# Hybrid decoder layer: where the gated norm's token scale is applied

## The chip, the cores and the metric

The kernel runs on one NeuronCore of a Trainium2 chip. The metric is the device time of one execution in microseconds (us); less is better. The engines are named as the profile names them: PE (TensorE: matmuls; PEld is its weight load), DVE (VectorE), ACT (ScalarE), POOL (GpSimd) and SP (SyncE, which here only issues DMAs). [...] The runs of the kernel before took 1358.45, 1358.78 and 1361.12 us, so the median is 1358.78 us.

## The reference, cut to what matters

One decoder layer is computed for 256 prompt tokens and 8 x 4 sample tokens, 288 columns in all, with D = 2048 features and fp32 accuracy. The part around the change is this (cut from the reference):

```python
h = rmsnorm(x, norm1) * (1 + sc1) + sh1
u_pool, z, xbc, dt_raw = split(h @ w_in)        # 512, 1536, 2560, 24 columns
pool_out = pool_mixer(u_pool)                   # 512 wide: window means minus the token, a 128x128 map per group
y = ssd(xbc, dt_raw) * silu(z)                  # 1536 wide
y = y * rsqrt(mean(y * y) + EPS) * ssd_norm     # gated RMSNorm: one factor for each token
mix = concat([pool_out, y]) @ w_out             # 2048 -> 2048
x = x + g1 * mix
h2 = rmsnorm(x, norm2) * (1 + sc2) + sh2        # then the gated MLP with a depthwise conv, and a final norm
```

The factor `rsqrt(mean(y*y)+EPS)` is one number per token. The matmul contracts over features, so that factor can be applied to `y` ahead of the projection, or to the projection's share of `y` behind it. The share of `pool_out` must not get it.

## The kernel before, in words

Features lie on the 128 partitions and the 288 tokens along the free axis, so an activation is 16 tiles of 128x288 (`KT = 16`) and a product is made per output tile `m` over the 16 tiles `k`. Every large product is made from fp32 operands that are each cut into two fp32r parts: `split` (L292) makes the parts `whi` (ACT, a cast, L288) and `wlo` (DVE, a subtraction, L290) of a weight block of eight `k`, and `mm3` (L300) issues three matmuls per `k`: high by high (L302), high weight by low activation (L303), low weight by high activation (L304). The activation's parts are `xhi[k]` and `xlo[k]`; `new_operand` takes 16 slots for each, so the tile `k` of a new operand takes the slot of the tile `k` of the operand before it, once the last matmul that reads it is through.

Weights come through SP as 512 KB blocks (`load`, L266), each into one of eight `raw` slots in this stage; a load waits on SP until a slot is free, and everything behind it on SP waits too. Blocks of the modulation weights (`raw_adap`, `ada_part_units`, L404) come through the same slots; their small matmuls (`adap`, L331) are filler work for PE, emitted by `pull(adas, ...)`.

The order of the work is the program's order, changed by the framework's scheduler: for every engine it makes one fixed list, from the program order, priorities (`tc.high_priority` in `split`) and its own estimate of when an operand is ready. On the chip each engine then works through its list and waits at its head for semaphores.

The stages around the change are these. The loop at L1047 makes the columns of `w_in` for `z` and for the last two pooling groups: `("uz", m)` for m = 10 to 15, then 1 and 0 (`ULATE`). Each unit of it is two `k` (`YK = 2`, six matmuls). Between units it steps the generators of other work: `late` (pooling, `pool_units`, L863), `adas`, and `back`, which holds the last parts of the state-space mixer (`ssd3`) and then `y_norm` (L902). `outputs` (L812) leaves the gated `y` in `zy[g]` (three tiles for each of four groups) and adds its squares on POOL into `ssq` (L839). `y_norm` sums `ssq` over the partitions by matmuls with ones (`ysum`, L240), takes the root and the reciprocal (L246, L247), spreads the result over the partitions by matmuls (`pbrstdy`, L253), copies it to SBUF (`rstdy`, L260), and multiplies all of `zy` by it (L908: three groups on DVE, one on POOL).

Behind that loop the weights of the first output tile are split, the pooling is finished, and the new operand `mix` is written: `mixh` on ACT with the gain `ssd_norm` as scale (L1081), `mixl` on DVE (L1082), for the 12 tiles of `y`; `mix_pool` (L1073) does it for the four pooling tiles. The projection runs over k in the order `MIXK`: 4 to 15 (the tiles of `y`), then 3, 2, 1, 0 (pooling). The loop at L1132 then makes 16 output tiles (`project_units`, L308; the PSUM tile `mm_out` is one of three buffers of `pm`). `residual` (L1095) adds the gated tile to `x` on DVE (256 prompt columns in one instruction, L1096; 32 sample columns, L1099) and POOL (L1102); `squares` starts the next norm. `x` is loaded again, four tiles at a time, by SP at L1135. Small PSUM tiles come from `aux`, four buffers.

The scratch pool `mx` (`zy`, `pout` and the rest) is closed at L1086, and `ff`, which holds `x`, takes its place; a tile of `ff` waits for the tiles of `mx` that lay there.

Of the kernel before, what the change touches and what calls it, by code (L numbers as in the profile page):

```python
# [18 lines left out]
P = 128  # L19
D = 2048  # L20
KT = D // P
# [39 lines left out]
HB = [(0, 3), (3, 3), (6, 2)]  # L61
KGROUPS = [(0, 1), (1, 1), (2, 2), (4, 4), (8, 4), (12, 4)]
MIXK = list(range(4, KT)) + UEARLY + ULATE
TW = (5, 3)
FK = 3
DGROUPS = [(0, 15), (15, 14), (29, 14)]
# [97 lines left out]
def kernel(ctx: ExitStack, tc, ins, outs):  # L164
# [14 lines left out]
    def aux(name):  # L179
        return px.tile([P, 512], F32, tag="aux", name=name)  # L180
# [708 lines left out]
        yield  # L889

    def uz_units(m):
        for ps in project_units(("uz", m), KT):
            yield
        if m < 4:
            nc.scalar.copy(upp[:, m, 15:15 + NP], ps[:, 0:NP])
            nc.scalar.copy(ups[:, m, :, 15:19], samp(ps[:, NP:N]))
        else:
            g, t = divmod(m - 4, 3)
            nc.scalar.activation(zy_of(g)[:, t, :], ps[:, :N], AF.Silu)
            zdone.add((g, t))  # L900

    def y_norm():  # L902
        psq = aux("ysum")
        col_sums(psq, ssq, ones[:, 0:1], True, True)
        rstdyp, rstdy = rstd_of(psq, NH * 64, "rstdy")
        yield
        for g in range(4):
            (nc.gpsimd if g == 3 else nc.vector).tensor_tensor(zy[g], zy[g],  # L908
                                    (rstdy if g else rstdyp).unsqueeze(1).to_broadcast([P, 3, N]), ALU.mult)
            yield  # L910


    def chain(*gens):
# [133 lines left out]
    for m in list(range(4 + 3 * ZEARLY, 16)) + ULATE:  # L1047
        for _ in uz_units(m):
            n += 1
            for gn in late.values():  # L1050
                pull(gn, 0.5)
            pull(adas, RA2 / AY)
            pull(back, RB2 if n <= zlast else RB3)
            if n == zlast:
                drain(back)
                back = chain(ssd3, y_norm())
        if m < 4:
            late[m] = pool_units(m)
            next(late[m])
    pull(adas, TA / AY)  # L1060
    for h, (_, n) in enumerate(_halves(KT)):
        ready[("out", 0, h)] = split(load(("out", 0, h)), 0, n * P, f"out_0_{h}")
    for gn in late.values():
        drain(gn)
    drain(back)
    npl = kp.tile([P, 4, 135], F32, tag="hmod", name="npl", bufs=2)
    nc.gpsimd.tensor_copy(npl[:, :, 0:15], upp[:, :, NP:15 + NP])
# [9 lines left out]
    for g in range(4):  # L1077
        for t in range(3):
# [2 lines left out]
            nc.scalar.activation(xhi[0][k], zy[g][:, t, :], AF.Identity, scale=gv)  # L1081
            nc.vector.scalar_tensor_tensor(out=xlo[0][k], in0=zy[g][:, t, :], scalar=gv,  # L1082
                                           in1=xhi[0][k].bitcast(F32), op0=ALU.mult, op1=ALU.subtract)
    for g in MIXK[12:]:
        mix_pool(g)
    mx_ctx.close()  # L1086
    ff = ctx.enter_context(tc.tile_pool(name="ff", bufs=1, reuse_waits="tile"))
    w2 = ctx.enter_context(tc.tile_pool(name="w2", bufs=1, reuse_waits="tile"))
    shift(w2, 192)
    x = ff.tile([P, KT, N], F32, name="x")  # L1090


    rt = [kp.tile([P, N], F32, tag="ssx", name="rt2")]

    def residual(ps, part, m):  # L1095
        nc.vector.scalar_tensor_tensor(out=x[:, m, 0:NP], in0=ps[:, 0:NP], scalar=ada[:, part, m, 0:1],  # L1096
                                       in1=x[:, m, 0:NP], op0=ALU.mult, op1=ALU.add)
        t = kp.tile([P, NB, NL], F32, tag="rsd", name=f"rs{part}_{m}", bufs=2)
        nc.vector.tensor_tensor(t, samp(ps[:, NP:N]),  # L1099
                                ada[:, part, m, 1:NC9].unsqueeze(2).to_broadcast([P, NB, NL]), ALU.mult)  # L1100
        xs = samp(x[:, m, NP:N])
        (nc.vector if m == KT - 1 else nc.gpsimd).tensor_tensor(xs, xs, t, ALU.add)  # L1102

    def squares(m, name):
        sq = kp.tile([P, N], F32, tag="xsq", name=f"sq{name}_{m}", bufs=2)
# [26 lines left out]
    for m in range(16):  # L1132
        if m in XM:
            sl = slice(4 * XM.index(m), 4 * XM.index(m) + 4)
            nc.sync.dma_start(x[:, sl, :], ins["x"][:, sl, :])  # L1135
        if m == 5:
            wp[0].add(w2, RAW2, SPLIT2)
        for i, ps in enumerate(project_units(("out", m), KT, order=MIXK)):
            if m == KT - 1 and i == 5:
                all_but_last("ssum2")  # L1140
        residual(ps, 2, m)
        squares(m, "a")
        pull(adas, (1 + (m >= 14 - ADA_OUT)) / AY)
        if m == 13:
            drain(adas)
# [20 lines left out]
    stf = ff.tile([P, FT, NB, 2], F32, name="stf")  # L1166
    nc.gpsimd.dma_start(stf, ins["st_ffn"])
    nff = ff.tile([P, FT, 18], F32, name="nff")
    NG = 2 + NP + NB * 6
    acts = {}  # L1170

    def up_pair(j):
# [124 lines left out]
def _layout(inp):  # L1297
    f = {k: np.asarray(v) for k, v in inp.items()}
    dt = f["w_in"].dtype
    xa = np.concatenate([f["x_prompt"][0], f["x_sample"].reshape(NS, D)], 0)  # L1300
    ca = np.concatenate([f["c_prompt"], f["c_sample"]], 0)
    r = {"x": _ftile(xa.T), "c": _ftile(ca.T)}

    early, vec = np.zeros((P, NE), dt), np.zeros((P, NV), dt)

    def put(o, a, to=vec):
        a = _ftile(a)
        a = a.reshape(P, -1)
        to[:, o:o + a.shape[1]] = a

    put(V_N1, f["norm1"][0], early); put(V_BADA, f["b_ada"][0], early)
    put(V_N2, f["norm2"][0]); put(V_NF, f["norm_f"])
    perm = np.concatenate([np.arange(t * P, t * P + P) for t in PERM])
    put(V_CW, f["conv_w"][0].T[perm]); put(V_CB, f["conv_b"][0][perm])
    put(V_SN, f["ssd_norm"][0]); put(V_PS, f["pool_scale"][0])
    put(V_FW, f["ffn_conv_w"][0].T); put(V_FB, f["ffn_conv_b"][0])
    put(V_D, np.repeat(f["d_skip"][0], 64))
    vec[:NH, V_DTB] = f["dt_bias"][0]
    vec[:NH, V_AL] = f["a_log"][0]
    r["early"], r["vec"] = early, vec  # L1320

    k = vec
    i = np.arange(P)
    early[:, K_ID:K_ID + P] = np.eye(P)
    k[:, K_TRI:K_TRI + 2 * P] = np.tile(i[:, None] <= i[None, :], (1, 2))
    l32, m32 = np.arange(32)[:, None], np.arange(32)[None, :]
    same = l32 // NL == m32 // NL
    k[:32, K_BT4:K_BT4 + P] = np.tile(same & (l32 <= m32), (1, 4))
    k[:32, K_BO4:K_BO4 + P] = np.tile(same, (1, 4))
    k[:, K_SEL:K_SEL + 32] = np.tile(np.eye(32), (4, 1))  # L1330
    k[:, K_MLO] = np.where(i // 64 == 1, -1.0, 0.0)
    k[:, K_MHI] = np.where((i // 32) % 2 == 1, -1.0, 0.0)
    k[:, K_BM4:K_BM4 + NB] = (i[:, None] % 32) // NL == np.arange(NB)[None, :]
    for g in range(4):
        k[:, K_RC + 16 * g:K_RC + 16 * g + 16] = 1.0 / np.minimum(np.arange(16) + 1, 2 << g)
    early[::32, K_S4] = 1.0
    early[:, K_S2:K_S2 + 64] = np.tile(np.eye(64), (2, 1))

    sc = _ftile(f["state_conv"][0].transpose(2, 0, 1)[perm]).reshape(P, -1)
    sp = _ftile(f["state_pool"][0].transpose(2, 0, 1)).reshape(P, -1)  # L1340
    r["st"] = np.ascontiguousarray(np.concatenate([sc, sp], 1))
    r["st_ffn"] = _ftile(f["state_ffn"][0].transpose(2, 0, 1))
    r["pool_w"] = np.ascontiguousarray(f["pool_w"][0].transpose(1, 0, 2))
    h = f["state_ssm"][0].reshape(NB, 4, HG, 64, P)
    r["h0"] = np.ascontiguousarray(h.transpose(0, 4, 1, 2, 3)).reshape(NB, P, 4, G6)

    w = np.empty(_STREAM.size, dt)

    def tiles(mat):
        return mat.reshape(mat.shape[0] // P, P, mat.shape[1] // P, P)  # L1350

    wa = f["w_ada"][0].reshape(KT, P, 6, KT, P)
    wi = f["w_in"][0]
    wuz = tiles(wi[:, 0:2048])
    wx = tiles(wi[:, 2048:4608])
    wx = np.concatenate([wx[:, :, PERM], wuz[:, :, UEARLY + list(range(4, 4 + 3 * ZEARLY))]], 2)
    wdt = wi[:, 4608:].reshape(KT, P, NH)
    wo, wu, wd = tiles(f["w_out"][0])[MIXK], tiles(f["w_up"][0]), tiles(f["w_down"][0])
    full = {"uz": (wuz, 0), "out": (wo, 0), "gate": (wu, 0), "val": (wu, FT)}
    for key in _STREAM.order:  # L1360
        o, cols = _STREAM.items[key]
        kind = key[0]
        if kind == "ada":
            k0, gk = KGROUPS[key[1]]
            per = RAWC // (256 * gk)
            s = wa[key[2] * per:(key[2] + 1) * per, :, 0:2, k0:k0 + gk]
            s = s.transpose(1, 0, 2, 3, 4)
        elif kind == "dt":
            s = wdt.transpose(1, 0, 2)
        elif kind == "adap":  # L1370
            s = wa[key[2], :, key[1], 8 * key[3]:8 * key[3] + 8]
        elif kind == "xbc":
            ks, ms = _xbc_chunks(key[1])[key[2]]
            s = wx[ks][:, :, ms].transpose(1, 2, 0, 3)
        elif kind == "upk":
            s = wu[key[1]][:, [m for j in range(FK) for m in (j, FT + j)]]
        elif kind == "down":
            k0, nk = DGROUPS[key[1]]
            a, n = _halves(nk)[key[3]]
            s = wd[k0 + a:k0 + a + n, :, key[2]].transpose(1, 0, 2)  # L1380
        else:
            mat, m0 = full[kind]
            a, n = _halves(KT)[key[-1]]
            s = mat[a:a + n, :, m0 + key[1]].transpose(1, 0, 2)
        w[o:o + P * cols] = s.reshape(-1)
    r["wflat"] = w
    return r
# [45 lines left out]
```

## Time and profile before

| What | Value |
|---|---|
| median of three runs | 1358.78 us |
| the profiled execution's own time | 1359.14 us |
| its span, first to last instruction | 1357.2 us |
| PE busy | 1340.9 us, 99% |
| DVE, ACT, POOL busy | 808.8, 580.3, 223.8 us |
| mean granted PE clock | 0.995 |
| DMA moved | 323.18 MB, mean 238 GB/s |

The profiled execution took 1359.14 us, 0.36 us over the median; 1.94 us of it lie outside the span. In the views of the profile a row has a start in us from the span's start, a duration in us, an engine, a line of the kernel, an operation and its tiles. Square brackets behind a row give the idle time ahead of it and what ended that. "PEclk" is the share of full clock that PE was granted. Times that a row gives for a group (x16) run from the first start to the last end.

### The profile page before, as it was taken

The numbers are of one execution on the slowest core, as the hardware profiler recorded it, in microseconds if no ns is written. First come the engines' busy times: TensorE is split into PE (matmuls) and PEld (weight loads), VectorE is DVE, ScalarE is ACT, GpSimd is POOL, SyncE is SP. The second block draws the span as 40 slices with busy tenths as digits, with TensorE's granted clock in tenths as the row PEclk, the third lists the DMA queues.
The fourth block names the chain that finished last, engine by engine and source line by source line (L and its number), as shares of the span: only waits on it lengthen the run. The fifth ranks groups of instructions, "written<-read, shape, count | busy, mean of one in ns | idle before, by whom it ended". The sixth has DMA issues, their size and how long they took to land.

```text
span 1357.2 us, 26159 instructions
## 1 busy us (share of the span) xinstructions
PE 1340.9 (99%) x10517; PEld 1249.0 (92%) x10517; DVE 808.8 (60%) x1348; ACT 580.3 (43%) x911; POOL 223.8 (16%) x435
## 2 busy tenths in 40 slices
PE   9999999999999999999999999999999999999997
PEld 8889997776779889999999999999999999999997
DVE  5675568778564348645565455656554556566553
ACT  5343244577543335534443334443433334444452
POOL 0000012123121213111211001311220011132221
PEclk9999999999999999999999999999999999999999
DMA  9999768878878878787555555655555555566541
GB/s 371 405 408 365 257 245 320 341 263 296 301 278 321 323 263 261 244 288 272 184 184 184 162 180 183 201 190 184 176 186 167 186 188 192 187 205 191 181 120 70
DMA packets 97481, 323.18 MB, mean 238 GB/s; under 512 B 10768, under 2 KB 19920, under 8 KB 97360
## 3 DMA queue, kind: packets, MB, share of 16 engines
q1 hardware_dynamic: 93600, 310.79, 66.1%
q0 software_dynamic: 3184, 9.69, 2.0%
q8 instruction: 82, 1.34, 0.4%
q10 hardware_dynamic: 576, 1.03, 0.2%
q14 instruction: 39, 0.32, 0.1%
HBM read 309.78 MB, written 10.39 MB: 236 GB/s over the span
## 4 chain that ended last, share of the span: by engine, by line
PE 74%; DVE 1%; issue 0%; POOL 0%; ACT 0%; DVEq 0%; POOLq 0%
PE mm_down L303 7%; PE mm_down L302 7%; PE mm_down L304 7%; PE mm_val L303 6%; PE mm_gate L303 6%; PE mm_gate L302 6%; PE mm_val L304 6%; PE mm_gate L304 6%; PE mm_val L302 6%; PE adap L331 3%; PE mm_out L302 3%; PE mm_out L303 3%; PE mm_out L304 3%; PE mm_up L303 1%; PE mm_up L302 1%; PE mm_up L304 1%
## 5 line engine op out<-in xcount | busy, mean ns | idle before, releaser
L303 PE MATMUL mm_down<-al,whi_down 128*128 128x288 f32 x688 | 202.5, 294 | 0.0
L302 PE MATMUL mm_down<-ah,whi_down 128*128 128x288 f32 x688 | 202.4, 294 | 0.0
L304 PE MATMUL mm_down<-ah,wlo_down 128*128 128x288 f32 x688 | 202.0, 294 | 0.0
L303 PE MATMUL mm_gate<-h2l,whi_gate 128*128 128x288 f32 x640 | 188.8, 295 | 0.0
L303 PE MATMUL mm_val<-h2l,whi_val 128*128 128x288 f32 x640 | 188.8, 295 | 0.0
L304 PE MATMUL mm_val<-h2h,wlo_val 128*128 128x288 f32 x640 | 188.7, 295 | 0.0
L304 PE MATMUL mm_gate<-h2h,wlo_gate 128*128 128x288 f32 x640 | 188.6, 295 | 0.0
L302 PE MATMUL mm_gate<-h2h,whi_gate 128*128 128x288 f32 x640 | 188.5, 294 | 0.0
L302 PE MATMUL mm_val<-h2h,whi_val 128*128 128x288 f32 x640 | 187.7, 293 | 0.0
L290 DVE TENSOR_TENSOR wlo_gate<-raw_gate,whi_gate 128x1024 fp32r<-128x1024 f32 x80 | 98.2, 1229 | 136.5 <-ACT whi_gate L288 136.3
L290 DVE TENSOR_TENSOR wlo_down<-raw_down,whi_down 128x1024 fp32r<-128x1024 f32 x96 | 107.5, 1120 | 116.9 <-ACT whi_down L288 116.9
L288 ACT CAST whi_down<-raw_down 128x1024 fp32r<-128x1024 f32 x96 | 92.5, 964 | 167.0 <-PE mm_down L303 117.8
L288 ACT CAST whi_gate<-raw_gate 128x1024 fp32r<-128x1024 f32 x80 | 84.2, 1054 | 159.7 <-PE mm_gate L303 66.9
L288 ACT CAST whi_val<-raw_val 128x1024 fp32r<-128x1024 f32 x80 | 84.2, 1053 | 120.8 <-issue 101.6
L302 PE MATMUL xbc<-h1h,whi_xbc 128*128 128x288 f32 x448 | 133.4, 301 | 0.8 <-ACT h1h L452 0.7
L303 PE MATMUL xbc<-h1l,whi_xbc 128*128 128x288 f32 x448 | 132.0, 296 | 0.0
L304 PE MATMUL xbc<-h1h,wlo_xbc 128*128 128x288 f32 x448 | 130.0, 295 | 0.0
L302 PEld LDWEIGHTS mm_down<-ah,whi_down 128*128 128x128 f32 x688 | 129.2, 188 | 0.0
L303 PEld LDWEIGHTS mm_down<-al,whi_down 128*128 128x128 f32 x688 | 129.1, 188 | 0.0
L304 PEld LDWEIGHTS mm_down<-ah,wlo_down 128*128 128x128 f32 x688 | 129.0, 188 | 0.0
L302 PEld LDWEIGHTS mm_gate<-h2h,whi_gate 128*128 128x128 f32 x640 | 120.3, 188 | 5.0 <-ACT ah L1198 3.4
L302 PEld LDWEIGHTS mm_val<-h2h,whi_val 128*128 128x128 f32 x640 | 120.3, 188 | 0.0
(325 smaller groups left out, 2983.4 us busy)
## 6 DMA issues: line engine op xcount, KB each, us to landing
raw_adap<-wflat SPq DMA_DIRECT2D x128, 512.0 KB, 6.1
raw_gate<-wflat SPq DMA_DIRECT2D x80, 512.0 KB, 3.5
raw_val<-wflat SPq DMA_DIRECT2D x80, 512.0 KB, 3.9
raw_ada<-wflat SPq DMA_DIRECT2D x64, 512.0 KB, 9.6
raw_xbc<-wflat SPq DMA_DIRECT2D x50, 512.0 KB, 9.1
raw_down<-wflat SPq DMA_DIRECT2D x48, 512.0 KB, 3.6
raw_out<-wflat SPq DMA_DIRECT2D x32, 512.0 KB, 7.4
raw_down<-wflat SPq DMA_DIRECT2D x32, 384.0 KB, 3.1
```

The source lines that it names most:

```text
L288: yield nc.scalar.copy(hi[:, :n], raw[:, a:a + n])
L290: yield hi, lo, nc.vector.tensor_tensor(lo[:, :n], raw[:, a:a + n], hi[:, :n].bitcast(F32), ALU.subtract)
L302: nc.tensor.matmul(ps, whi[:, w], bh, start=first, stop=False)
L303: nc.tensor.matmul(ps, whi[:, w], bl, start=False, stop=False)
L304: nc.tensor.matmul(ps, wlo[:, w], bh, start=False, stop=last)
L331: nc.tensor.matmul(ps[32 * j:32 * j + 32, :nb], sc_c[:, k, :], raw[:, c:c + nb], start=(k == 0), stop=(k == KT - 1), tile_position=(0, 32 ...
```

## The change

`y_norm` goes. The operand `mix` is made from the unscaled `zy`, with only the gain `ssd_norm`. The sum of squares, the root and the spreading of the token factor (the first half of `y_norm`) are issued inside the first output tile, behind its fourth unit; the last pooling work and the four `mix_pool` behind its second unit. Each output tile now accumulates in two PSUM tiles: the first 12 of its 16 `k` (the features of `y`) in `pz` from `pm`, the last four (pooling) in `pp` from `aux`. When the 12 are through, `out_norm` multiplies `pz` by `rstdy` on DVE into an SBUF tile and adds that to `x` by `residual`; when the tile is through, `residual` runs a second time for `pp`. The number of matmuls stays the same. The last `("uz", 0)` tile walks its `k` in the order `MIXK`, so that the slots of h1's tiles 4 to 15 become free first, and its weights are laid out in that order on the host. The first output tile is issued ahead of `mx_ctx.close()`, and with it ahead of the first load of `x`.

```diff
+NZ = 12
     def uz_units(m):
-        for ps in project_units(("uz", m), KT):
+        for ps in project_units(("uz", m), KT, order=MIXK if m == ULATE[-1] else None):
             yield
-    def y_norm():
-        psq = aux("ysum")
-        col_sums(psq, ssq, ones[:, 0:1], True, True)
-        rstdyp, rstdy = rstd_of(psq, NH * 64, "rstdy")
-        yield
-        for g in range(4):
-            (nc.gpsimd if g == 3 else nc.vector).tensor_tensor(zy[g], zy[g],
-                                    (rstdy if g else rstdyp).unsqueeze(1).to_broadcast([P, 3, N]), ALU.mult)
-            yield
...
                 drain(back)
-                back = chain(ssd3, y_norm())
+                back = ssd3
...
-    for gn in late.values():
-        drain(gn)
     drain(back)
...
-    for g in MIXK[12:]:
-        mix_pool(g)
+
+    def out_units(m):
+
+        pz = pm.tile([P, 512], F32, tag="mm", name=f"mm_out_{m}")
+        pp = aux(f"mm_outp_{m}")
+        for h, (k0, n) in enumerate(_halves(KT)):
+            hi, lo = ready.pop(("out", m, h), None) or split(load(("out", m, h)), 0, n * P, f"out_{m}_{h}")
+            for i in range(n):
+                k = k0 + i
+                mm3((pz if k < NZ else pp)[:, :N], hi, lo, i, xhi[0][MIXK[k]], xlo[0][MIXK[k]],
+                    k in (0, NZ), k in (NZ - 1, KT - 1))
+                if k % YK == YK - 1:
+                    yield pz, pp
+
+    out0 = out_units(0)
+    for i in range(KT // YK):
+        ps0 = next(out0)
+        if i == 1:
+            for gn in late.values():
+                drain(gn)
+            for g in MIXK[NZ:]:
+                mix_pool(g)
+        if i == 3:
+            psq = aux("ysum")
+            col_sums(psq, ssq, ones[:, 0:1], True, True)
+            _, rstdy = rstd_of(psq, NH * 64, "rstdy")
     mx_ctx.close()
...
+    NG = 2 + NP + NB * 6
...
+    def out_norm(pz, m):
+        t = ff.tile([P, NG], F32, tag="gc", name=f"oz{m}", bufs=2)[:, :N]
+        nc.vector.tensor_tensor(t, pz[:, :N], rstdy, ALU.mult)
+        residual(t, 2, m)
...
-        for i, ps in enumerate(project_units(("out", m), KT, order=MIXK)):
-            if m == KT - 1 and i == 5:
-                all_but_last("ssum2")
-        residual(ps, 2, m)
+        if m == 0:
+            out_norm(ps0[0], m)
+        else:
+            for i, (pz, pp) in enumerate(out_units(m)):
+                if m == KT - 1 and i == 5:
+                    all_but_last("ssum2")
+                if i == NZ // YK - 1:
+                    out_norm(pz, m)
+        residual(ps0[1] if m == 0 else pp, 2, m)
         squares(m, "a")
...
+            if key[:2] == ("uz", ULATE[-1]):
+                mat = mat[MIXK]
```

More of the change, by code (lines that the diff above doesn't have):

```diff
@@ L1168 @@
     nff = ff.tile([P, FT, 18], F32, name="nff")
-    NG = 2 + NP + NB * 6
     acts = {}
```

## The prediction, on record before the changed kernel ran

> **What bounds the kernel now.** I read the page's first lines, then busy time by stage, then PE's waits, then PE's clock around them.
>
> ```profile
> span 1357.2 us, 26159 instructions
> PE 1340.9 (99%) x10517; PEld 1249.0 (92%) x10517; DVE 808.8 (60%) x1348; ACT 580.3 (43%) x911; POOL 223.8 (16%) x435
> ```
>
> ```profile
> 360.00:392.00 32.00, 28.77 (x185) 20.99 (x181) 22.40 (x47) 14.60 (x31) 5.98 (x11) 0.89 0.75 280
> 392.00:1340.00 948.00, 948.00 (x7164) 924.76 (x7163) 531.80 (x795) 381.71 (x548) 174.29 (x342) 1.00 0.62 205
> ```
>
> The columns of the second fence are the stretch, its length, busy PE, PEld, DVE, ACT and POOL, then the granted clock, the DMA share and GB/s. PE is the bound: 1340.9 of 1357.2 us. From 392 to 1340 us it never rests and has full clock, so whatever this change does to DVE or ACT there is free while PE stays fed, and a PE that arrives earlier at 392 ends earlier by as much. The change moves matmuls and removes none. What it can win lies in 360 to 392, where PE works 28.77 of 32.00 us and has 0.89 of its clock.
>
> ```profile
> PE mm_out L303 <- DVE mixl L1082: 2.0, 1, 2.0
> PE ysum L240 <- POOL ssq L839: 1.2, 1, 1.2
> ```
>
> ```profile
> 364.57:367.98 3.41, 2.21 (x18) 1.98 (x17) 3.38 (x10) 1.97 (x5) 1.42 (x1) 1.00 0.89 306
> 367.98:371.40 3.42, 3.42 (x17) 3.42 (x16) 0.09 (x1) 0.24 (x1) 0.00 (x0) 0.51 0.98 386
> 371.40:374.81 3.41, 3.41 (x26) 3.22 (x25) 3.21 (x3) 2.29 (x5) 2.06 (x1) 0.99 0.12 47
> 374.81:378.22 3.41, 3.38 (x27) 0.76 (x25) 3.41 (x7) 3.41 (x9) 1.45 (x3) 1.00 0.34 70
> 378.22:381.63 3.41, 1.41 (x8) 1.22 (x9) 3.41 (x12) 2.94 (x8) 0.00 (x0) 1.00 0.97 357
> 381.63:385.05 3.42, 3.42 (x11) 1.61 (x9) 3.37 (x8) 0.44 (x1) 0.41 (x1) 0.51 1.03 420
> ```
>
> Two waits of PE, 1.2 and 2.0 us, and right behind the 3.41 us stretch that holds each of them one such stretch at half clock (0.51). A stretch of small `adap` matmuls (374.81) is followed by full clock, so filler work does not cost the clock; rest does. A shorter rest elsewhere did not:
>
> ```profile
> 286.21 0.37 PE L800 MATMUL cse<-csr,selr 128*128 128x288 f32 x1 [0.96 <-DVE ada L419]
> ```
> ```profile
> 288.40:291.80 3.40, 3.40 (x33) 1.61 (x32) 3.21 (x5) 2.94 (x5) 0.00 (x0) 1.00 0.77 263
> ```
>
> So a wait above some 1 us has so far cost itself and up to 3.42 x 0.49 = 1.68 us more.
>
> [...]
>
> **The change part by part.** What made the two waits:
>
> ```profile
> 364.79 1.42 POOL L839 TENSOR_TENSOR ssq<-ssq,ysq 128x288 f32<-128x288 f32 x1 [4.67 <-ACT ysq L835]
> ```
> ```profile
> 371.60 1.05 DVE L908 TENSOR_TENSOR zy<-zy,pbrstdy 128x864 f32<-128x864 f32 x1 [3.53 <-ACT rstdy L260]
> 372.57 3.01 DVE L908 TENSOR_TENSOR zy<-zy,rstdy 128x864 f32<-128x864 f32 x2
> 377.78 1.21 DVE L290 TENSOR_TENSOR wlo_out<-raw_out,whi_out 128x1024 fp32r<-128x1024 f32 x1
> 379.66 0.51 DVE L1082 SCALAR_TENSOR_TENSOR mixl<-zy,vec,mixh 128x288 fp32r<-128x288 f32 x1
> 382.11 3.52 DVE L1082 SCALAR_TENSOR_TENSOR mixl<-zy,vec,mixh 128x288 fp32r<-128x288 f32 x8
> ```
>
> POOL adds the last squares until 366.21, and PE stands at `ysum` for them, with the `uz` matmuls behind it. DVE then idles 3.53 us for the token factor, scales `zy` until 375.58, and has two weight subtractions (one shown) and pooling ahead of the first `mixl` at 379.66. PE waits for that.
>
> (1) `ysum` moves behind 24 matmuls of the first output tile, long after `ssq` is done: that wait goes, 1.20, and with it the half clock, 1.68. (2) `mix` no longer needs the factor. `zy` is done when its last squares are added (364.79), and walking `k` in `MIXK` order frees the slots of tiles 4 and up first; DVE's idle 3.53 us takes most of the 12 `mixl`. The wait of 2.03 goes, and its half clock, 1.68. Sum: 1.20 + 1.68 + 2.03 + 1.68 = 6.6 us. The matmuls of `ysum` and its spreading run later, unchanged: 0.
>
> What is late next:
>
> ```profile
> 363.18 0.30 PE L302 MATMUL mm_uz<-h1h,whi_uz 128*128 128x288 f32 x1
> 374.41 0.60 PE L342 MATMUL adat_p<-early,asb_p 128*128 128x128 f32 x4
> 374.94 1.92 PE L331 MATMUL adap<-raw_adap,sc_c 128*32 128x512 f32 x16
> 377.12 1.07 PE L331 MATMUL adap<-raw_adap,sc_c 128*32 128x512 f32 x8
> 383.33 1.91 PE L331 MATMUL adap<-raw_adap,sc_c 128*32 128x512 f32 x2
> ```
> ```profile
> 367.89 0.17 DVE L882 TENSOR_TENSOR pout<-pout,upp 128x16 f32<-128x16 f32 x1
> ```
> ```profile
> 391.00:495.00 104.00, 104.00 (x792) 94.38 (x792) 46.13 (x66) 38.61 (x48) 22.66 (x32) 1.00 0.84 309
> ```
> ```profile
> 362.59 0.86 SPq L269 DMA_DIRECT2D raw_out<-wflat  x2
> ```
>
> (a) Pooling in the last `uz` tile. The tile's 48 matmuls start at 363.18 (the 48th row back from its end). A matmul takes 104.00 / 792 = 0.131 us apiece at full clock, so its fourth unit ends at 363.18 + 24 x 0.131 = 366.3. There the pooling matmul of group 1 can stand in PE's list, and its operand is ready at 368.06. Before, it stood behind `ysum` and hid. Bounds 0 and 1.7 us; a list made by readiness, as before, puts it later, so 0.3.
>
> (b) Transfers. Without the wait, the half clock and the two moved steps the `uz` tile needs 48 x 0.131 = 6.3 us and an estimated 0.6 for the pooling matmul: `adat_p` comes at 370.1, not 374.41, 4.3 us sooner. All eight `raw` slots are full then (DMA share 0.12 in 371.40:374.81), and the next loads wait for the 16 `adap` matmuls at 374.94. So loads come 4.3 us sooner, but PE wants to be 6.6 sooner at the end of the tile.
>
> ```profile
> 376.03 0.80 SPq L269 DMA_DIRECT2D raw_adap<-wflat  x2
> ```
> ```profile
> DMA to landing us min/median/max: 3.9/6.3/13.2
> ```
>
> The `adap` block issued at 376.03 is used at 383.33, 7.3 us on; its landing is 3.9 to 6.3 us after the issue. At the same place of the list PE would come 1.85 + 1.0 + 17 x 0.131 = 5.1 us after the 16 matmuls' start, and the block is there 1.1 + 3.9 to 6.3 = 5.0 to 7.4 us after it. Bounds 0 and 2.3 + 1.68 = 4.0 us with half clock; in the middle of both, weighed for a list that puts the filler later, 1.5. Tile 0's weights are asked for at 362.59 and used from 370.1 + 0.5 + 1.9 + 1.0 = 373.5 on; nothing there.
>
> (c) DVE in the first tile. From 368.06 on it has 12 `mixl` at 3.52 / 8 = 0.44 (5.3), two `wlo_out` at 1.21 (2.4), the rest of pooling (some 2, an estimate), four more `mixl` (1.8) and tile 1's first `wlo_out` (1.2): 12.7 us, until 380.8. PE wants the pooling tiles from 373.5 + 36 x 0.131 and some 3 us of other matmuls on, about 381. Nearly even. Bounds 0 and the 2.03 us that the same kind of wait took; 0.5, because `mixl` starts 11 us earlier and each `k` needs only one.
>
> (d) The root inside the tile. ACT has to load the root's table again:
>
> ```profile
> 365.01 1.28 ACT L246 ACT_TABLE_LOAD   x1
> ```
>
> Before, it hid in ACT's wait for `ysum`; now between casts. PE's spreading matmuls wait for root and reciprocal. Bounds 0 and 1.3; ACT is idle in that stretch once `mixh` is made, so 0.1.
>
> [...]
>
> (e) Each tile's second half on DVE:
>
> ```profile
> L655 DVE TENSOR_TENSOR cvp<-cvp,xbc 128x288 f32<-128x288 f32 x76 | 32.8, 452 | 31.1 <-PE xbc L304 30.8
> ```
> ```profile
> L1096 DVE SCALAR_TENSOR_TENSOR x<-mm_out,ada,x x16: 477/484/486, 394.0 to 499.9; 128x256 f32<-128x256 f32 x16
> L1099 DVE TENSOR_TENSOR rs<-mm_out,ada x16: 180/181/184, 396.6 to 500.3; 128x32 f32<-128x32 f32 x16
> ```
> Per tile one multiply out of PSUM (0.45), one L1096 (0.48), one L1099 (0.18) and one more small add on POOL: 1.1 us x 16 = 17.8 us of DVE. DVE is busy 46.13 of 104.00 us there (391.00:495.00), so it goes to some 62%; PE's cover is whole. Cost 0. If the cover went, it would be at the last tile:
>
> ```profile
> 500.49 0.54 ACT L1107 ACTIVATE sqa<-x 128x256 f32<-128x256 f32 x2 [6.20 <-DVE rs L1099]
> ```
> ```profile
> 501.65 0.83 PE L240 MATMUL ssum<-ones,sqa 128*128 128x1 f32 x6
> ```
>
> The squares are done at 501.03 and PE takes them at 501.65, behind fillers: 0.6 us of slack. The tile's `y` part is ready 12 x 0.131 = 1.6 us ahead of its end and takes 1.3 us with the final add on DVE, so it fits; at worst 0.7 us.
>
> Gone are 4.06 us of DVE (371.60 to 375.58) and the POOL product beside it; their worth is in (2).
>
> **Sum:** 6.6 - 0.3 - 1.5 - 0.5 - 0.1 = 4.2 us. The profiled execution took 1359.14 us (span 1357.2 and 1.94 around it), so 1354.9; the median of the runs is 0.36 lower, which gives 1354.6. A measurement of this kernel tells about 0.2%, 2.7 us.
>
> **The rivals.** *All of it:* filler and pooling are listed late enough, the costs stay near 0.4 us: 1358.8 - 6.2 = 1352.6. For it: no work is added to PE. Against: DMA moves only 4.3 us.
>
> *Nothing measurable:* a new wait over 1 us brings back one half-clock stretch. (b) at 4.0, (a), (c) and (d) together 0.9 as above: 6.6 - 4.9 = 1.7 gained, 1357.1. The change also fails to do what it says if the first `mixl` is still late in DVE's list. It comes out alike if the half-clock stretches are not due to the waits and stay: then 1.20 + 2.03 = 3.2 us can be won and some 1.6 of the costs remain, 1357.2; two stretches right behind two waits make that unlikely, 0.05 of this rival's chance. [...]
>
> *Slower, by `x`:* the first load of `x` is issued behind the first tile now.
>
> ```profile
> 380.05 0.98 SPq L1135 DMA_DIRECT2D x<-x  x2
> ```
> ```profile
> x<-x SPq DMA_DIRECT2D x2, 576.0 KB, 12.3
> ```
> ```profile
> 391.75 1.05 ACT L288 CAST whi_out<-raw_out 128x1024 fp32r<-128x1024 f32 x1 [3.85 <-PE mm_out L303]
> ```
> ```profile
> 393.98 0.48 DVE L1096 SCALAR_TENSOR_TENSOR x<-mm_out,ada,x 128x256 f32<-128x256 f32 x1
> ```
>
> Issued at 380.05, landed 12.3 us later at 392.4, used at 393.98; tile 0's last matmuls are through at about 391.7, when ACT gets their weight slot. `residual` of tile 0 on DVE now comes earlier, and if it waits for `x`, tile 1's second weight subtraction waits behind it. PE would need that at about 385.1 + 24 x 0.131 + 0.5 = 388.7 (385.1: tile 0's end, 391.7, less 6.6). With `x` landing at L it is done at L + 0.48 + 1.22, so PE waits L - 387.0. Moved 4.3 us with the other loads, L is 388.1 and the wait 1.1. If the load also waits for the scratch tiles that the first output tile still reads, it goes out at about 381 to 384 and lands at 390.7 to 395.9: waits of 3.7 to 8.9 us and one or two half-clock stretches. At L = 394 that is 7.0 + 3.4 + 0.9 of other costs, less 6.6: 4.7 slower, 1363.5; it is slower by over 0.2% from about L = 392 on. For it: a DVE at its limit in (c), and a DMA share of 0.97 to 1.03 from 378 on. Against: before, the load went out while `mix` was still being read.
>
> **How the numbers follow.** Forecast 0.38 (own range 1353.4 to 1356.3), all of it 0.2, nothing measurable 0.2, slower 0.22. Faster by over 0.2%: 0.38 + 0.2 = 0.58; within 0.2%: 0.2; slower: 0.22. Range: down to 1351.8 (the full 6.6, and small costs turned round), up to 1363.0, which leaves about 0.1 of the slower cases above it.
>
> **What would show it.** Right: no `ysum` wait and no wait for `mixl` in PE's waits; clock 1.00 in all stretches from 360 to 392; the first `mixl` before 370; `rstdy` behind 375; 17 us more DVE in the projection and PE still without a wait there. (b) wrong or right: PE waiting at `adap` in 372 to 385. Slower: DVE idle ahead of tile 0's `residual` for the load of `x`, then PE idle for `wlo_out`. The prediction falls if a PE wait over 1 us stands in tiles 0 to 2, or if PE waits recur per tile.

## The result and the profile after

The changed kernel took 1353.36 us (median of five runs, 1353.11 to 1354.27) against 1358.78 us for the kernel before: a ratio of 0.9959, 95% interval 0.9945 to 0.9972. That is 5.4 us less. Measured once more on another occasion it took 1353.55 us, 0.9963 (0.9949 to 0.9977). The profiled execution of the changed kernel took 1353.11 us, 6.0 less than the profiled one before.

The first lines of the page of the changed kernel, and busy time by stage (columns as in the prediction):

```profile
span 1351.3 us, 26246 instructions
PE 1337.3 (99%) x10517; PEld 1247.5 (92%) x10517; DVE 820.0 (61%) x1394; ACT 579.4 (43%) x911; POOL 227.5 (17%) x449
```
```profile
363.00:392.00 29.00, 28.21 (x206) 23.73 (x205) 21.28 (x50) 16.24 (x32) 5.11 (x11) 1.00 0.91 349
392.00:1335.00 943.00, 943.00 (x7124) 919.79 (x7123) 542.20 (x836) 378.77 (x546) 179.25 (x355) 1.00 0.62 204
```

PE now rests 0.79 us from 363 to 392 and has its full clock there. Behind 392 DVE does 542.20 us of work instead of 531.80, in a stretch 5 us shorter, and PE still never rests. PE's three largest waits, and one more that the kernel before does not list:

```profile
PE warm L229 <- DVE ones L194: 1.1, 1, 1.1
PE cse L801 <- DVE ada L420: 1.0, 1, 1.0
PE pool L888 <- DVE pout L883: 0.8, 1, 0.8
PE dttr L582 <- DVE dtt L570: 0.6, 1, 0.6
```

The waits at `ysum` and `mixl` are gone. Two are new. The one at `dttr` lies at 213 us, ahead of the stages that were changed; e6 and e7 below, which share that part, show 0.2 and 0.6 us for it, and the `uz` stage starts only 0.2 us later than before. The one that the change makes is at the pooling matmul. PE's and then DVE's and SP's rows around it, from the timeline:

```profile
369.10 0.72 PE L888 MATMUL pool<-pout,poolw 128*128 128x288 f32 x2 [0.79 <-DVE pout L883]
371.77 1.93 PE L332 MATMUL adap<-raw_adap,sc_c 128*32 128x512 f32 x16
378.59 1.04 PE L332 MATMUL adap<-raw_adap,sc_c 128*32 128x512 f32 x2
380.15 0.72 PE L241 MATMUL ysum<-ones,ssq 128*128 128x1 f32 x6
380.81 1.92 PE L332 MATMUL adap<-raw_adap,sc_c 128*32 128x512 f32 x14
382.66 0.85 PE L254 MATMUL pbrstdy<-early,r3rstdy 128*128 128x128 f32 x6
```
```profile
367.85 0.51 DVE L1071 SCALAR_TENSOR_TENSOR mixl<-zy,vec,mixh 128x288 fp32r<-128x288 f32 x1
368.36 0.50 DVE L1071 SCALAR_TENSOR_TENSOR mixl<-zy,vec,mixh 128x288 fp32r<-128x288 f32 x1
368.79 0.16 DVE L883 TENSOR_TENSOR pout<-pout,upp 128x16 f32<-128x16 f32 x1
383.98 0.46 DVE L1120 TENSOR_TENSOR oz<-mm_out,rstdy 128x288 f32<-128x288 f32 x1 [0.24 <-ACT rstdy L261]
389.36 1.22 DVE L291 TENSOR_TENSOR wlo_out<-raw_out,whi_out 128x1024 fp32r<-128x1024 f32 x1 [1.39 <-ACT whi_out L289]
390.50 0.48 DVE L1110 SCALAR_TENSOR_TENSOR x<-oz,ada,x 128x256 f32<-128x256 f32 x1
```
```profile
382.27 1.88 SPq L1154 DMA_DIRECT2D x<-x  x2
```

`mixl` starts at 367.85, 11.8 us earlier than before. Two `mixl` now stand in DVE's list between the pooling operations (367.85 and 368.36), so pooling's last step is at 368.79, where it had been at 367.89, and PE waits for it. `ysum` and `pbrstdy` lie between other matmuls.

Where the time went can be followed by the first and last start of two groups of matmuls, before and then after:

```profile
L302 PE MATMUL mm_uz<-h1h,whi_uz x128: 288/295/509, 257.5 to 374.0; 128*128 128x288 f32 x128
L302 PE MATMUL mm_up<-h2h,whi_upk x96: 289/295/398, 506.9 to 544.9; 128*128 128x288 f32 x96
```
```profile
L303 PE MATMUL mm_uz<-h1h,whi_uz x128: 290/295/509, 257.7 to 370.9; 128*128 128x288 f32 x128
L303 PE MATMUL mm_up<-h2h,whi_upk x96: 289/295/401, 500.9 to 538.9; 128*128 128x288 f32 x96
```

The `uz` stage is 3.3 us shorter (116.5 to 113.2). By the terms: 1.20 + 1.68 for the first wait, less 0.79 for the new one, and 1.3, an estimate, for the matmuls of `ysum` and `pbrstdy`, which moved out of the stage: 1.20 + 1.68 - 0.79 + 1.3 = 3.4. From the last `uz` to the first `up` it is 2.9 us shorter (132.9 to 130.0): 2.03 + 1.68, less the 1.3 that moved in, is 2.4. The other 0.5 I can't assign. Behind 506.9 (500.9) nothing more is won or lost beyond 0.2 us.

### The profile page after: what moved, and what is told of

It is laid out like the page before. It is cut to its first block, busy times and chain, and to the rows that moved or that the text cites. A ratio compares the mean times of both kernels' runs of the same rounds, so it can differ in the third digit from the quotient of the medians.

```text
span 1351.3 us, 26246 instructions
## 1 busy us (share of the span) xinstructions
PE 1337.3 (99%) x10517; PEld 1247.5 (92%) x10517; DVE 820.0 (61%) x1394; ACT 579.4 (43%) x911; POOL 227.5 (17%) x449
## 4 chain that ended last, share of the span: by engine, by line
PE 74%; DVE 1%; issue 0%; ACT 0%; DVEq 0%
PE mm_down L304 7%; PE mm_down L303 7%; PE mm_down L305 7%; PE mm_gate L303 6%; PE mm_val L304 6%; PE mm_gate L304 6%; PE mm_val L305 6%; PE mm_gate L305 6%; PE mm_val L303 6%; PE adap L332 3%; PE mm_out L303 2%; PE mm_out L304 2%; PE mm_out L305 2%; PE mm_up L303 1%; PE mm_up L304 1%; PE mm_up L305 1%
## 5 line engine op out<-in xcount | busy, mean ns | idle before, releaser
L289 ACT CAST whi_gate<-raw_gate 128x1024 fp32r<-128x1024 f32 x80 | 83.8, 1049 | 160.0 <-PE mm_gate L304 64.9
L305 PEld LDWEIGHTS mm_gate<-h2h,wlo_gate 128*128 128x128 f32 x640 | 120.5, 188 | 0.0
```

What stands on the lines that cost most here:

```text
L289: yield nc.scalar.copy(hi[:, :n], raw[:, a:a + n])
L305: nc.tensor.matmul(ps, wlo[:, w], bh, start=False, stop=last)
```

## The experiments

Two theories stood against each other. Mine: the gain is the two waits with their half-clock stretches, each by its own part of the change. The other: only the operand (`mixl` no longer waiting for the factor) matters, and the rest of the change is decoration or costs.

**e1: only the place of the sum.** The changed kernel, with `ysum` back in the last `uz` tile (`y_sum` holds the lines that are taken out below):

```diff
-                back = ssd3
+                back = chain(ssd3, y_sum())
...
-        if i == 3:
-            psq = aux("ysum")
-            col_sums(psq, ssq, ones[:, 0:1], True, True)
-            _, rstdy = rstd_of(psq, NH * 64, "rstdy")
+    rstdy = ybox[0]
```

> The changed kernel with one part put back: the sum of squares, root and spreading stand in the last uz tile again, where the kernel before had them; the operand stays unscaled and the factor is applied behind the projection. PE's list has 13 uz matmuls, then the three ysum matmuls, as before. Theory (waits plus clock): PE waits 1.2 us for the last squares again and gets one stretch of 3.41 us at half clock behind it, +1.2 +1.7, while the 0.8 us wait of the pooling matmul goes, since it then stands behind the spreading: about +2.1 us on the changed kernel, 1355.5. Rival A (only the waits count, half clock has another cause): +0.4, 1353.8. Rival B (the gain is from the mixl wait alone): 1353.4, no difference.

It took 1356.22 us (1355.42 to 1357.61), 0.9982 (0.9973 to 0.9991) of before: 2.5 us over e2 below, which ran beside it. PE's waits, and its clock around the first of them:

```profile
PE ysum L241 <- POOL ssq L840: 1.2, 1, 1.2
PE mm_out L305 <- DVE wlo_out L291: 0.7, 1, 0.7
PE mm_out L303 <- ACT whi_out L289: 0.6, 1, 0.6
```
```profile
363.32:366.73 3.41, 2.40 (x19) 2.17 (x17) 1.75 (x2) 3.17 (x7) 1.29 (x1) 1.00 0.86 308
366.73:370.15 3.42, 3.24 (x26) 3.24 (x27) 3.15 (x12) 2.19 (x5) 0.13 (x1) 1.00 0.94 337
```

The wait for `ssq` came back, so the place of the sum does take it away. But the clock stayed full: the border of a stretch, at 366.73 (stretches counted in steps of 3.413 us), cut this wait of 1.19 us (365.72 to 366.91) into 1.01 and 0.18. And two waits at the start of tile 3, counted from 0 (0.63 us at 401.48, 0.74 at 402.74) came up that the changed kernel hasn't. With the 0.79 at the pooling matmul gone, these waits make 1.19 + 1.37 - 0.79 = 1.8 of the 2.5 us; the rest is not assigned. The size was near what I had thought, its parts were not.

**e2: the order of `k` in the last `uz` tile.** The `MIXK` order of that tile and of its weights is undone:

```diff
-        for ps in project_units(("uz", m), KT, order=MIXK if m == ULATE[-1] else None):
+        for ps in project_units(("uz", m), KT):
```

> The changed kernel with only the order of k in the last uz tile put back to 0 to 15 (and its weights' layout with it). The lists of PE and ACT are the same; the slots of h1's tiles 4 to 15 become free 4 steps of 0.4 us later, so each mixh on ACT can start up to 1.6 us later, and the first weight cast of the output tile behind them by about 1.3. Theory that the order matters: PE waits about 1 us for the first wlo of the output tile, 1354.3, or 1356 if a half-clock stretch follows. Rival (the order is not needed, the operand has time to spare): 1353.4.

1353.71 us (1352.88 to 1354.31), 0.9961 (0.9948 to 0.9973): the same as the changed kernel. PE's list was the same too, with the wait of 0.8 at the pooling matmul. This part of the change is not needed for the gain, and the reason that term (2) of the prediction gave for it, slots that become free first, wasn't needed either.

**e3: one PSUM tile, no scaling behind it.** This kernel leaves the token factor out of the result.

```diff
-        pp = aux(f"mm_outp_{m}")
+        pp = pz
...
-                if i == NZ // YK - 1:
-                    out_norm(pz, m)
```

> The changed kernel with all 16 k in one PSUM tile and one residual per output tile; the token factor is computed but not applied, so this part of the computation is left out. It takes away the 16 multiplies and 16 second residuals, 17.8 us of DVE. Theory (that DVE work lies wholly beside PE): 1353.4 within 0.7 us. Rival (the added DVE work costs PE time per tile): faster by 0.1 to 0.3 us for each of 16 tiles, 1349 to 1352.

1355.14 us (1354.56 to 1355.84), 0.9974 (0.9963 to 0.9984): slower than with the extra DVE work, by 1.4 us against e2 beside it. Busy time by stage, and the two PE waits that were new, from the timeline:

```profile
392.00:1335.00 943.00, 941.70 (x7113) 918.21 (x7112) 529.20 (x791) 377.95 (x544) 174.57 (x339) 1.00 0.61 204
```
```profile
400.77 0.40 PE L303 MATMUL mm_out<-mixh,whi_out 128*128 128x288 f32 x1 [0.56 <-ACT whi_out L289]
402.03 0.40 PE L305 MATMUL mm_out<-mixh,wlo_out 128*128 128x288 f32 x1 [0.74 <-DVE wlo_out L291]
```

13.0 us less DVE work won nothing. The lists came out another way, and 0.56 + 0.74 = 1.3 us of waits at the start of tile 3, the place at which e1 had them too, are about the difference of 1.4. That the extra work costs nothing on PE's path rests on this sum and on the changed kernel itself, where PE has no rest from 392 to 1335 us with all of the work.

**e4: the kernel before, without the products with the factor.** The other theory by itself; the result lacks the factor here too:

```diff
-        for g in range(4):
-            (nc.gpsimd if g == 3 else nc.vector).tensor_tensor(zy[g], zy[g],
-                                    (rstdy if g else rstdyp).unsqueeze(1).to_broadcast([P, 3, N]), ALU.mult)
-            yield
```

> The kernel before with only the three DVE products and the one POOL product left out that scale zy by the token factor; the factor is still computed where it was, but not applied, so this part of the computation is left out. Theory: the ysum wait of 1.2 us and its half-clock stretch stay, the mixl wait of 2.0 us and its half-clock stretch go: -3.7 us, 1355.1, and one split filler group less (0.9), 1354.2. Rival A (half clock has another cause): -2.0, 1356.8, or 1355.9 without the split. Rival B (the next thing, ACT waiting for the spread factor ahead of mixh, is as late as mixl was): 1358.8.

1356.63 us (1354.54 to 1357.72), 0.998 (0.9971 to 0.9989): 2.1 us less than before, not 5.4. The wait for `mixl` was gone; the one for `ysum` (1.19 us, from 365.28 to 366.47) stayed, and this time it lay whole in one stretch, with the half clock in the next:

```profile
364.58:367.99 3.41, 2.22 (x18) 1.99 (x17) 3.41 (x10) 2.99 (x8) 1.42 (x1) 1.00 1.03 422
368.00:371.41 3.41, 3.41 (x18) 3.41 (x16) 1.44 (x6) 0.87 (x3) 0.00 (x0) 0.50 0.89 358
```

The 1356.63 us is nearly the 1356.8 that stood for Rival A, half clock with another cause. The rows say otherwise: of the two half-clock stretches that the kernel before has from 360 to 392 us only the one behind `ysum` is left, and the mean clock there is 0.95 instead of 0.89; the other went with the `mixl` wait. What my theory's 1354.2 left out stands in PE's waits: this list has some for weight splits in tiles 2 and 3, 0.20 + 0.73 + 0.56 + 0.73 = 2.2 us, in the place of the 2.03 us for `mixl`, and 1354.2 + 2.2 is 1356.4. The larger part of them:

```profile
PE mm_out L304 <- DVE wlo_out L290: 1.5, 2, 0.7
```

So the operand alone gave less than half, and the other theory falls on the row: the wait at `ysum` stays without the rest of the change. How much the operand would give in a list without the 2.2 us, e4 can't tell.

**e5: the pooling matmul half a tile later.** To see if the 0.79 can be had:

```diff
-                pull(gn, 0.5)
+                pull(gn, 0.25 if m == ULATE[-1] else 0.5)
```

> The changed kernel with one edit: the pooling matmul stands half a tile later in the order, behind the last matmul of the last uz tile, where its operand pout (written by VectorE at 368.79 in the changed kernel) has long been there. Theory (the 0.79 us that the pooling matmul waited in the changed kernel is term (a), and it is on the path): the wait goes, nothing takes its place, 1353.36 - 0.79 = 1352.6 us, with the matmuls of the stages behind it 0.7 to 0.8 us earlier. Rival (another wait of about the same length comes up in the list that follows, as with the single bank): 1353.1 to 1353.6 us. A rival on the other side: the chain pool -> root -> ysum scale ends later by half a tile (1.7 us) and the first eviction of tile 0 waits for it: over 1354 us.

1353.6 us (1352.83 to 1353.75), 0.9963 (0.995 to 0.9975): no gain. The wait at `pool` was gone, and PE's waits had this instead:

```profile
PE mm_out L305 <- DVE wlo_out L291: 0.7, 1, 0.7
```

The rival was right: the 0.8 us went into a wait of 0.71 us for a late weight subtraction, at 374.58, in the first output tile (in e1 and e3 it was tile 3).

**e6 and e7: the filler's groups kept whole.** The rows of `adap` above show that two of these small matmul rows take 1.04 us and fourteen 1.92. Eight make one group (four column strips, two rows each), and a group takes about as long cut as whole: 1.04 us for the two rows, 1.06 for eight in e6 below. The edit holds each group together in PE's list; e7 adds the edit of e5:

```diff
+            glue = begun or j > js[0]
+            with tc.high_priority() if glue else nullcontext():
...
+            if glue:
+                tc.keep_in_program_order(i)
...
-            for h in range(2):
+            for h in (1, 0):
```

> The changed kernel with one edit: the four matmuls of each column group of the modulation vectors (adap), which run side by side in four column strips, are held together in the list, also where the scheduler would place them two by two as their halves arrive. Lists of the trace are cut into 72 groups where 64 would do; with the edit there are 66. Theory (a group that is cut in two costs one more group, 0.93 us, since two rows take as long as eight: in the changed kernel x2 took 1.04 us and x14 1.92): 6 groups x 0.93 = 5.6 us less, about 1348 us. Rival (a whole group has to wait for the later of its two halves' loads, and TensorE then stands for it): waits of mm_out or adap for raw_adap of 1 to 2 us each, 1351 to 1356 us.

> The two edits together: the pooling matmul behind the last uz tile, and the groups of the modulation vectors held together. If the two costs are separate and both on TensorE's path they add: 1353.36 - 0.8 - 5.6 = 1347.0 us. If the order that the one gives takes away the other's wait or makes a new one: 1348 to 1353 us.

> The changed kernel once more, beside the kernel with both edits on the same chip: 1353.4 us, 0.9959 of the kernel before.

> The kernel with both edits once more, beside the changed kernel on the same chip. If its gain of 2.4 us over the changed kernel is one of the kernel and not of the chip: 1351.0 us against 1353.4. If it was the chip's (the two were measured on different occasions): within 1 us of each other.

e6 took 1351.38 us (1349.96 to 1351.78), 0.9944 (0.993 to 0.9958) of before; e7 1351.0 us (1349.72 to 1351.78), 0.9944 (0.9931 to 0.9956). Once more beside the changed kernel on one chip, e7 took 1350.41 us (1349.6 to 1351.86) against 1353.55 (1353.45 to 1353.96): 3.1 us less, so the gain is one of the kernel. Rows of e6 where the changed kernel had 2 and 14, then its waits that are new:

```profile
376.33 1.06 PE L334 MATMUL adap<-raw_adap,sc_c 128*32 128x512 f32 x8
378.57 1.06 PE L334 MATMUL adap<-raw_adap,sc_c 128*32 128x512 f32 x8
```
```profile
PE mm_up L303 <- ACT h2h L457: 1.3, 2, 0.8
PE ssum L924 <- ACT sq L920: 1.0, 1, 1.0
PE y L821 <- ACT ec L811: 1.0, 1, 1.0
PE xbc L305 <- DVE wlo_xbc L291: 0.5, 1, 0.5
```

Up to 420 us, e6 has 42 such groups where the changed kernel has 47: six lists became whole and one near 215 us came out cut once more. Over the whole run the `adap` matmuls keep PE busy for 64.9 us instead of 70.1, 5.2 us less, near the 5.6 that was expected of six groups. Against e5, which ran beside it, the waits shown add 3.8 and PE's other listed waits are 1.3 less in sum, which leaves 2.7; measured were 2.2. The price of a cut group fits to 0.5 us, but waits took half of it, as the rival had it, though at other places than it named. Both e6 and e7 beat the kernel before and the changed one; e7's further edit is not told apart from e6.

**p1 and p2: when does the clock halve?** Because e1 kept its clock and e4 lost it behind the same wait, I put probes into the three down stages of the changed kernel, with PE held to program order there: chains that make PE rest for a known time, and in p2 also rows of one-column matmuls:

```diff
+    def probe(name, n, w):
+        with tc.high_priority():
+            pr = aux("pr" + name)
...
+            nc.tensor.matmul(pr[:, P:2 * P], t, ones, start=True, stop=True)
+            for _ in range(w):
+                nc.tensor.matmul(pr[:, 300:301], ones, ones[:, :1], start=True, stop=True)
```

> A measurement of the granted clock: the changed kernel with 24 small chains added to the three stages of the down projection (matmul, then 1 to 8 VectorE operations on 128x128 of about 0.28 us each, then a matmul that waits for the last of them), so that TensorE rests for about 0.5 to 2.5 us at known places. The time is longer by the rests and is not compared; the output is the reference's. Theory (the granted clock is halved for one stretch of 3.413 us when the stretch before it holds more than about 1.0 to 1.2 us of rest, whatever its place): rests of under 1 us never halve it, rests of 1.2 us or more halve it when they fall into one stretch and not when the border of a stretch cuts them into two parts under 1 us each. Rival A (only a stretch that is at rest from border to border halves it): none of these rests does. Rival B (any rest above about 1.1 us halves it, wherever it falls): no rest that a border cuts is spared.

> A second measurement of the granted clock, with other probes in the same places of the changed kernel; its time is not compared. First down stage: no rest at all, but 4 to 16 matmuls of one column (128x1, the shape of ysum, about 0.23 us each) in a row. Second: a rest of 1.31 us each time, followed by 0 to 7 such matmuls. Third: a rest of 1.96 us eight times, at whatever place of the stretch it falls. Theory (a stretch of 3.413 us halves the clock of the next one when rest and one-column matmuls in it come to more than 1.85 us together; so far 1.82 us of pure rest did not, 1.94 did, and 1.20 of rest with 0.69 of ysum did): in the first stage rows of 9 and more (2.1 us) halve it, if they lie in one stretch; in the second 3 or more (1.31 + 0.69 = 2.0) do and none and one do not; in the third every probe that lies within one stretch halves it and those that a border cuts do not. Rival (one-column matmuls count as work, and 1.20 us of rest halved the clock for another reason): no half clock in the first two stages at all.

Two rests of p1, each whole inside one stretch, and the clock of that stretch and the next:

```profile
1343.78 0.49 PE L1273 MATMUL pr<-ones,prt 128*128 128x128 f32 x2 [1.69 <-DVE prt L1272]
1357.61 0.49 PE L1273 MATMUL pr<-ones,prt 128*128 128x128 f32 x2 [2.02 <-DVE prt L1272]
```
```profile
1341.90:1345.31 3.41, 1.72 (x14) 1.53 (x13) 1.94 (x6) 0.30 (x1) 0.00 (x0) 1.00 0.38 124
1345.31:1348.72 3.41, 3.41 (x28) 3.41 (x27) 1.33 (x3) 1.95 (x4) 1.20 (x2) 1.00 0.26 52
1355.55:1358.96 3.41, 1.40 (x11) 1.35 (x11) 1.89 (x7) 0.11 (x1) 0.00 (x0) 1.00 0.36 115
1358.97:1362.38 3.41, 3.41 (x16) 3.41 (x15) 1.51 (x3) 1.58 (x3) 1.18 (x2) 0.50 0.22 43
1089.31:1092.72 3.41, 1.59 (x12) 1.59 (x13) 1.86 (x7) 0.40 (x1) 0.00 (x0) 1.00 0.48 157
1092.73:1096.14 3.41, 3.41 (x28) 3.41 (x27) 1.30 (x3) 1.07 (x2) 0.25 (x1) 1.00 0.23 50
```

Up to 1.82 us of rest in a stretch (3.41 less 1.59) left the next at full clock; from 1.94 on all of them halved it (2.01 in the one shown, 3.41 less 1.40). In p2 the eight rests of the third stage were seven times 2.0 us and once 1.7, and a border cut every one of them (stretches counted from 1066.45 in steps of 3.413 us), with 1.63 us at most on one side: none halved the clock. One of them, the stretch with its larger part, and the next:

```profile
1392.35 0.49 PE L1278 MATMUL pr<-ones,prt 128*128 128x128 f32 x2 [2.01 <-DVE prt L1277]
```
```profile
1390.72:1394.13 3.41, 1.78 (x13) 1.79 (x14) 1.90 (x8) 0.56 (x1) 0.00 (x0) 1.00 0.00 0
1394.13:1397.54 3.41, 3.41 (x28) 3.41 (x27) 1.08 (x3) 1.94 (x4) 1.18 (x2) 1.00 0.02 5
```

One-column matmuls, rows and stretches of p2:

```profile
1051.72 0.50 PE L1280 MATMUL pr<-ones 128*128 128x1 f32 x4
1065.29 0.73 PE L1280 MATMUL pr<-ones 128*128 128x1 f32 x6
```
```profile
1052.81:1056.21 3.40, 3.40 (x28) 3.40 (x27) 1.57 (x3) 0.85 (x2) 0.25 (x1) 1.00 0.20 43
1066.45:1069.86 3.41, 3.41 (x16) 3.41 (x15) 1.54 (x3) 0.83 (x1) 1.03 (x1) 0.50 0.05 7
779.73:783.14 3.41, 3.41 (x16) 3.41 (x15) 1.23 (x3) 0.94 (x1) 0.25 (x1) 0.50 0.24 96
```

A rest of 1.31 us with two of them behind it (1.81 in all) kept the clock, with three (2.04) it halved. Ten of them in a row, 2.29 us with no rest at all in that stretch, halved it too; nine (2.07 us) didn't, against my 1.85. So they count as rest, or nearly: a row's length overlaps the matmuls beside it by some 0.15 us (the nine start at 763.16, the next matmul at 765.09), which is too coarse to tell. The rivals on record fall: a stretch need not rest from border to border, the border does spare a wait, and one-column matmuls do not count as work. My own limit for p1 falls with them: I had put it at 1.0 to 1.2 us, and rests of 1.3 to 1.8 us kept the clock.

The 1.20 us wait of `ysum` fits this: with an estimated 0.69 us of one-column matmuls behind it (three at the 2.07 / 9 us of the nine), it makes 1.89 us in its stretch, between the 1.82 that kept the clock and the 1.94 that halved it.

## Why the prediction was right

- What bounds the kernel: right. PE had no rest behind 392 us in either kernel, and what it gained ahead of it stayed gained.
- (1), the `ysum` wait: right as far as the wait goes; e1 shows it return. Its half clock of 1.68 was taken as certain, and it isn't: it came with the same wait in e4 and not in e1. Of 23 runs of the kernel before that were measured beside e1 to e4, five had a mean clock of 0.995, as the profiled one (both half-clock stretches), 16 had 0.996 and two 0.997 (one such stretch lowers the mean by 3.413 x 0.5 / 1357 = 0.0013); their medians were 1359.60, 1358.46 and 1358.59 us. The mean also holds a half-clock stretch at the end of the span, 5.7 to 8.6 us long in the kept traces. With an end like that, 0.996 leaves room for one other such stretch and 0.995 for two, so the usual run of the kernel before seems to have one, not two. The medians of the two groups are 1.1 us apart, not 1.7, so this is a reading, not shown. The profiled executions differ by 6.0, the medians by 5.4. The prediction took both stretches from the one run that was profiled.
- (2), the `mixl` wait: right; the first `mixl` is at 367.85, and e4 takes this wait away without the rest of the change. The order of `k` had no part in it (e2).
- (a), pooling in the last `uz` tile: 0.79 measured where 0.3 was taken, inside its bounds. The list made by readiness did put it late, behind 36 matmuls, but the `mixl` that start early now stand ahead of its operand on DVE.
- (b), the transfers: 1.5 was taken, none was paid. This is the term that was mis-sized. I kept the second `adap` block at the same place of the list, 5.1 us behind the start of the first; the list has it behind 36 matmuls of the first output tile, and its main part runs at 380.81, 9.0 us behind 371.77. I had named this case and still took 1.5 of the 4.0 us that were at stake. The transfer was quick as well: the first of the block's two loads went out at 372.87 and landed 3.9 us later, at 376.8, which is 5.0 us behind 371.77 and just ahead of the place that I had assumed.
- (c) and (d): 0.5 and 0.1 were taken, none was paid on PE. The root waits on ACT for `ysum` as before, and `oz` waits 0.24 us on DVE for it, with PE fed.
- (e), DVE work in each output tile: right, nothing; e3 shows that without it no time is won. It added less to DVE than the 17.8 us that I gave it: DVE is busy for 820.0 us, and for 804.9 in e3, 15.1 less.
- The sum: 6.6 of gains less 2.4 of costs was taken. In the profiled execution the gains came near 6.6, and the costs were 0.8. The result lies between the forecast and "all of it", by mechanism nearer to the latter. That the number came so close has some luck in it: half of the 6.6 was half clock, which not every run of the kernel before seems to have in full, and the costs were put 1.6 us too high; for the median the two errors work against each other.
- "Slower, by `x`": the load did go out late, at 382.27, in the 381 to 384 that I gave for it. But DVE's list has the second weight subtraction of tile 1 (389.36) ahead of the part of tile 0's residual that reads `x` (390.50), so a late load held nothing that PE needed. The assumption that it stands behind was the weak step of this rival. Its second step was off too: the load landed 6.7 us after its issue, at 389.0, not at 390.7 to 395.9.
- "Nothing measurable": no new wait of over 1 us came. The half-clock stretches went with the waits, so its second form falls as well.

The half-clock stretches shown here, ahead of the end of the span, were 3.41 us long each, and within a run they start whole steps of 3.413 us apart: 779.73 and 1066.45 in p2 are 286.72 us apart, 84 steps, and 367.98 and 381.63 in the kernel before are 13.65 us apart, four steps.

## What to carry to other kernels

Look at a wait of TensorE by what it adds to the rest of its 3.41 us stretch, short matmuls with one column included: here 0.12 us (1.82 or 1.94) decided over 1.7 us more, and so did the border of the stretch (the same 1.19 us kept the clock in e1 and halved it in e4). When work moves, ask the engine's new list for its place instead of keeping the old place, since the scheduler moves the filler as well. And a wait that is taken away by order alone may come back at the next operand that is nearly late: here it was the weight split of tiles 0, 2 or 3, in four of the experiments (e1, e3, e4 and e5).

## What the runs showed of the hardware

In p1 the clock of TensorE was halved for 3.41 us behind every stretch with 1.94 us of rest or more, and behind none with 1.82 or less. In p2 a rest that the border of a stretch cut was spared (2.01 us, of which 1.63 in one stretch). Matmuls 128x1 counted as rest, or nearly: in p2, 1.31 us of rest and 0.50 of them kept the clock, 1.31 and 0.73 halved it, and of them alone 2.07 us didn't halve the clock and 2.29 did. Two rows of a group of `adap` matmuls in column strips took 1.04 us (the changed kernel) and eight 1.06 (e6), so splitting such a group between two places of the list costs about a whole group more, half of the 1.92 us that sixteen took in the kernel before.
